# First norm of a decoder step: k-tiles 0 and 1 as two stages of their own with half granules, and the other k-tiles scaled on GpSimd

## The chip, the core and the metric

The kernel runs on one core of a Trainium2 chip. The metric is device microseconds of one execution, the median of several runs. TensorE (PE) does the matmuls, VectorE (DVE), ScalarE (ACT) and GpSimd (POOL) the elementwise work, and SyncE (SP) issues most of the DMA transfers.

## What is computed

One step of a recurrent decoder layer for 256 prompt tokens and 32 sample tokens (8 sequences of 4), 288 columns in all, in fp32. The part that the change touches is the beginning:

```python
mod = jax.nn.silu(c) @ P['w_ada'] + P['b_ada']
sh1, sc1, gt1, sh2, sc2, gt2 = [m[:, None, :] for m in jnp.split(mod, 6, axis=-1)]
xn = rmsnorm(x, P['g_norm1']) * (1.0 + sc1) + sh1
mix, st = mixer(xn, states[l], P)      # begins with proj = xn @ P['w_in']
```

`x` has 2048 features, 16 k-tiles of 128. `c` has nine rows (one for the prompt, eight for the samples), and `w_ada` is 2048 x 12288; of it the first norm needs the columns of `sc1` and `sh1`, 32 MB. The three mixer branches, the output projection, a second norm, a feed-forward part of width 8192 and a last norm follow.

## The kernel before

Features lie on partitions and tokens along the free axis. Every large product is a `stream` (L160): four PSUM tiles of 128 output features x 288 columns, fed by granules of the weight. A granule is two k-tiles by 512 output features, 512 KB. `fetch` (L151) issues its DMA on SyncE and then splits it: ScalarE writes the rounded `hi` (L156), VectorE the rest `lo = raw - hi` (L157). For each k-tile and each of the four output tiles there are three matmuls: hi by xh (L171), hi by xl (L172), lo by xh (L173); xh and xl are the same split of the input. raw, hi and lo have three buffers each. SyncE issues in program order; the order on the other engines is made by a scheduler from priorities, `issue_after` and a simulated time line.

The first norm is not finished before the streams begin. The weights of `sc1` and `sh1` come in 32 units of 1 MB (`first`, L317), ordered by stages: `STAGES` (L26) gives for each stage the k-tiles whose modulation it needs. Stage 0 is k-tiles 0 and 1 (4 units), then 2 and 3 (4 units), 4 to 7, 8 to 11, 12 to 15 (8 units each). A unit's product (L275) is many small matmuls into one PSUM tile; the last unit of a stage is followed by `by_feature` (a transpose, L237) and `ada_finish` (L297, L300), which write `mod`. `modulate` (L404) then scales and shifts the stage's k-tiles in place, prompt columns by L409, sample columns by L412, and splits them into xh (L420) and xl (L421).

Per stage, six streams run (`early`: the projections for q, k, v and the first branch), each over the k-tiles of this stage alone. In stage 0 the PSUM tile is copied to its slot by VectorE and ScalarE in turn (`first_part`, L467), and in all later stages VectorE adds it (`plus_slot`, L472). Between two granules a pattern of letters (L477) says what is put in: L loads the next unit, V multiplies (visits) all units that are loaded, a point does nothing. A stage asserts that its units were visited.

Ahead of all this, squares of x are summed (L430, L432, L434), `rs` is the reciprocal root (L391 to L395), and VectorE multiplies x by `rs` in five instructions (L442), k-tiles 0-1, 2-3, 4-7, 8-11 and 12-15. Four units are loaded with the first granule behind the third, and visited one by one (L455 to L461). The tile `par` of small parameters comes in one transfer on GpSimd's queue (L95), of `con` only `eye` at first; the rest of `con` is loaded by GpSimd after a copy that waits for `mod` (L488 to L490).

Of the kernel before, what the change touches and what calls it, by code (L numbers as in the profile page):

```python
# [8 lines left out]
F32 = mybir.dt.float32  # L9
F32R = mybir.dt.float32r  # L10
AF = mybir.ActivationFunctionType
ALU = mybir.AluOpType
# [12 lines left out]
SH1, SC1, GT1, SH2, SC2, GT2 = range(6)  # L25
STAGES = [(0, 2, 0), (2, 4, 4), (4, 8, 8), (8, 12, 16), (12, 16, 24)]  # L26
NPRE = 6
# [3 lines left out]
          ("glo", 128), ("causal", 128), ("bdm", 128), ("hsel", 4), ("head", 4), ("half", 2)]  # L31
PARAMS = [("lcw", 32), ("lcb", 8), ("mcw", 32), ("mcb", 8), ("ba", 8), ("bx", 8), ("lam", 8),
# [21 lines left out]
def trunk(ctx, tc, io):  # L54
# [39 lines left out]
    par = cp.tile([P, PW], F32, tag="par", name="par")  # L94
    G.dma_start(par, io["par"])  # L95

# [48 lines left out]
    def weight_tiles():  # L145
        at["n"] += 1
        return [weight_tile(n) for n in ("raw", "hi", "lo")]
# [3 lines left out]
    def fetch(w, blk, g, kg=2, ahead=True):  # L151

        with tc.high_priority() if ahead else nullcontext():
            raw, hi, lo = (t.rearrange("p (k m) -> p k m", k=kg) for t in weight_tiles())
            Q.dma_start(raw, w[blk, g].rearrange("p (k m) -> p k m", k=kg))
            pace["hi"] = S.activation(hi, raw, AF.Copy)  # L156
            pace["lo"] = V.tensor_tensor(out=lo, in0=raw, in1=hi.bitcast(F32), op=ALU.subtract)  # L157
        return hi, lo

    def stream(w, blk, act, kt, evac, g0=0, width=512, ahead=True, k0=0, kg=2):  # L160
# [3 lines left out]
        for g in range(k0 // kg, kt // kg):  # L164
            hi, lo = fetched.pop(0) if fetched else fetch(w, blk, g0 + g, kg, ahead)
            for m in range(nm_t):
# [237 lines left out]
    def modulate(k0, k1, step):  # L404

        for k in range(k0, k1, step):
            x, r = (xa, xb)[k // 8][:, k % 8:k % 8 + step], slice(k, k + step)
# [31 lines left out]
    rs = inv_sqrt(row("lf"), ps[:, :N], bias=eps, scale=1.0 / (32 * D))  # L439
    for k, n in ((0, 2), (2, 2), (4, 4), (8, 4), (12, 4)):  # L440
        t = (xa, xb)[k // 8][:, k % 8:k % 8 + n, :]
        V.tensor_tensor(out=t, in0=t, in1=rs.unsqueeze(1).to_broadcast([P, n, N]), op=ALU.mult)  # L442

# [10 lines left out]

    slots.update(ids=(8, 9, 2, 3), n=0)  # L455
    for i in range(4):
        if i == 3:
            fetched.append(fetch(win, B_Q, 0))
        load_one()
    for i in range(4):  # L460
        visit(1)  # L461
# [8 lines left out]
    def plus_slot(dst, base):  # L470
        def f(m, p):
            V.tensor_tensor(out=dst[:, base + m, :], in0=dst[:, base + m, :], in1=p, op=ALU.add)  # L472
        return f


    slots.update(ids=(4, 5, 6, 7, 3, None, "st"), n=0)
    for i, p in enumerate((". L L L LV .", "L LL LL LV LLV .", "L L . L LV . L L . LLV . .", "L L . L LV . L L . LLV . .", "L L L L . V . L L . V .")):  # L477
        k0, k1, _ = STAGES[i]
        assert i < 4 or not held
        if i == 4:  # L480
            slots.update(ids=(3, 4, None, 5, 6, 7), n=0)
        every(p)
        assert f"first{i}" in done
        with tc.high_priority():
            modulate(k0, k1, 2 if i else 1)
        if i == 0:
            a, w = COFF["eye"]
            for r in (slice(0, a), slice(a + w, CW)):  # L488
                G.tensor_copy(con[:, r.start:r.start + 1], mod[:, SC1, 0, 0:1])
                G.dma_start(con[:, r], io["con"][:, r])  # L490
# [1108 lines left out]
```

## Time and profile before

| | us |
|---|---|
| median of 3 runs | 1980.41 |
| lowest and highest | 1979.29, 1980.63 |
| profiled execution, its own time | 1981.87 |
| its span | 1980.1 |
| TensorE busy in the span | 1942.9 |

A row of the timeline gives the start, the duration, the engine, the line of the kernel, the operation with out<-in and shape, a count where like instructions follow each other, and in brackets the idle time of the engine ahead of it with what ended it. Durations overlap where an engine is pipelined; the distance of two starts is then the price of one. PEclk is the granted TensorE clock as a share of 2.4 GHz.

### The profile page before, as it was taken

The page shows a single profiled execution, that of the slowest core. Times are in us where ns is not written, and L with a number is a line of the kernel's source. Part 1 is how long each engine was busy: PE and PEld are TensorE (multiplying, and loading weights), DVE is VectorE, ACT ScalarE, POOL GpSimd, SP SyncE. Part 2 cuts the span into 40 slices and gives each one's busy share as a digit, 9 for nine tenths or more (in the row PEclk, how much of TensorE's full clock was granted, in tenths as well). Part 3 has the DMA queues.
Part 4 walks back from the last instruction along what each step waited for, and adds up shares of the span by engine and source line. Part 5 has one row for each costly group of instructions (what it writes and reads, how often), then busy time and mean ns, then how long its engine had stood idle before and what let it go on. Part 6 is the DMA issues. An engine that isn't in the chain of part 4 may idle for free.

```text
span 1980.1 us, 35638 instructions
## 1 busy us (share of the span) xinstructions
PE 1942.9 (98%) x14944; PEld 1839.8 (93%) x14944; DVE 1048.5 (53%) x1582; ACT 810.8 (41%) x1128; POOL 233.7 (12%) x319
## 2 busy tenths in 40 slices
PE   6999999999999999999999999999999999999997
PEld 5899989998999998799999999999999999999997
DVE  5665747545673456554444564444444445454565
ACT  4232464535454344243333454443333334343433
POOL 0000200000133021101013331000000001010101
PEclk8999999999999999999999999999999999999999
DMA  9887757537543358957778645444444444444443
GB/s 381 331 306 287 293 196 271 205 140 263 186 152 134 122 180 274 313 202 276 276 280 348 245 146 191 160 166 163 173 170 160 160 164 172 168 162 166 160 162 120
DMA packets 109569, 416.99 MB, mean 211 GB/s; under 512 B 11569, under 2 KB 11745, under 8 KB 105697
## 3 DMA queue, kind: packets, MB, share of 16 engines
q1 hardware_dynamic: 100368, 382.34, 52.5%
q0 software_dynamic: 8032, 28.99, 4.4%
q10 hardware_dynamic: 1008, 3.39, 0.5%
q8 instruction: 117, 1.92, 0.4%
q14 instruction: 44, 0.35, 0.1%
HBM read 397.86 MB, written 16.81 MB: 209 GB/s over the span
## 4 chain that ended last, share of the span: by engine, by line
PE 95%; DMA 3%; DVE 1%; issue 1%; ACT 0%; SPq 0%; DVEq 0%; POOL 0%; ACTq 0%; POOLq 0%
PE mm L171 28%; PE mm L173 28%; PE mm L172 28%; PE pa L275 4%; DMA raw<-win 2%; PE px L1256 0%; PE pi L1248 0%; DMA st<-gla 0%; DVE lo L157 0%; PE px L573 0%; DMA s<-mC 0%; PE px L804 0%; PE px L1183 0%; PE px L128 0%; PE px L652 0%
## 5 line engine op out<-in xcount | busy, mean ns | idle before, releaser
L157 DVE TENSOR_TENSOR lo<-raw,hi 128x1024 fp32r<-128x1024 f32 x450 | 555.8, 1237 | 545.6 <-ACT hi L156 528.1
L156 ACT ACTIVATE hi<-raw 128x1024 fp32r<-128x1024 f32 x450 | 476.9, 1061 | 826.4 <-PE mm L172 621.7
L171 PE MATMUL mm<-xh,hi 128*128 128x288 f32 x2576 | 763.2, 300 | 6.4 <-ACT xh L420 6.2
L172 PE MATMUL mm<-xl,hi 128*128 128x288 f32 x2576 | 760.2, 297 | 0.1
L173 PE MATMUL mm<-xh,lo 128*128 128x288 f32 x2576 | 744.7, 296 | 0.7 <-DVE lo L157 0.6
L171 PEld LDWEIGHTS mm<-xh,hi 128*128 128x128 f32 x2576 | 483.6, 189 | 26.1 <-issue 9.9
L171 PE MATMUL mm<-s,hi 128*128 128x288 f32 x1664 | 490.7, 297 | 0.3 <-ACT s L936 0.3
L172 PEld LDWEIGHTS mm<-xl,hi 128*128 128x128 f32 x2576 | 486.3, 189 | 2.7 <-issue 0.9
L172 PE MATMUL mm<-s,hi 128*128 128x288 f32 x1664 | 488.6, 295 | 0.0
L173 PEld LDWEIGHTS mm<-xh,lo 128*128 128x128 f32 x2576 | 481.5, 189 | 3.3 <-DVE lo L157 1.4
L173 PE MATMUL mm<-s,lo 128*128 128x288 f32 x1664 | 476.4, 295 | 0.4 <-DVE lo L157 0.4
L171 PEld LDWEIGHTS mm<-s,hi 128*128 128x128 f32 x1664 | 311.8, 188 | 5.7 <-issue 4.6
L172 PEld LDWEIGHTS mm<-s,hi 128*128 128x128 f32 x1664 | 312.5, 188 | 0.8 <-issue 0.5
L173 PEld LDWEIGHTS mm<-s,lo 128*128 128x128 f32 x1664 | 308.3, 188 | 1.3 <-DVE lo L157 0.7
L157 DVE TENSOR_TENSOR lo<-s,hi 128x1024 fp32r<-128x1024 f32 x80 | 98.0, 1225 | 113.8 <-ACT hi L156 113.8
L156 ACT ACTIVATE hi<-s 128x1024 fp32r<-128x1024 f32 x80 | 85.0, 1062 | 140.7 <-PE mm L172 140.0
L1432 POOL TENSOR_TENSOR t<-t 128x288 f32<-128x288 f32 x64 | 60.2, 951 | 639.2 <-ACT t L1431 639.2
L472 DVE TENSOR_TENSOR s<-s,mm 128x288 f32<-128x288 f32 x96 | 41.8, 451 | 41.3 <-PE mm L173 40.4
L275 PE MATMUL pa<-s,silc 128*32 128x128 f32 (+2 forms) x720 | 53.3, 411 | 5.9 <-DMA s<-wad 5.9
L1448 DVE TENSOR_TENSOR s<-s,mm 128x288 f32<-128x288 f32 x96 | 40.3, 451 | 33.8 <-PE mm L173 32.6
L955 POOL TENSOR_TENSOR s<-s,t 128x288 f32<-128x288 f32 x32 | 30.8, 989 | 190.3 <-DVE t L954 190.2
L275 PEld LDWEIGHTS pa<-s,silc 128*32 128x32 f32 x720 | 21.8, 112 | 23.6 <-issue 10.3
(379 smaller groups left out, 1123.4 us busy)
## 6 DMA issues: line engine op xcount, KB each, us to landing
raw<-win SPq DMA_DIRECT2D x192, 512.0 KB, 4.7
raw<-wf SPq DMA_DIRECT2D x176, 512.0 KB, 4.1
s<-wf SPq DMA_DIRECT2D x80, 512.0 KB, 3.3
s<-wada SPq DMA_DIRECT2D x26, 1024.0 KB, 8.8
s<-wad SPq DMA_DIRECT2D x24, 1024.0 KB, 8.5
ag<-wada SPq DMA_DIRECT2D x22, 1024.0 KB, 5.5
raw<-wout SPq DMA_DIRECT2D x32, 512.0 KB, 5.7
st<-wada SPq DMA_DIRECT2D x20, 512.0 KB, 7.6
```

What stands on the lines that cost most here:

```text
L156: pace["hi"] = S.activation(hi, raw, AF.Copy)
L157: pace["lo"] = V.tensor_tensor(out=lo, in0=raw, in1=hi.bitcast(F32), op=ALU.subtract)
L171: T.matmul(pss[m][:, :N], hi[:, kk, ms], xh, start=k == k0, stop=False)
L172: T.matmul(pss[m][:, :N], hi[:, kk, ms], xl, start=False, stop=False)
L173: pace["last"] = T.matmul(pss[m][:, :N], lo[:, kk, ms], xh, start=False, stop=k == kt - 1)
L275: pace["prod"] = T.matmul(ps[32 * j:32 * j + 32, h * w // 4:(h + 1) * w // 4], silu_c(k), v[:, j], start=k == 0 and h == 0, stop=k == KT - ...
L472: V.tensor_tensor(out=dst[:, base + m, :], in0=dst[:, base + m, :], in1=p, op=ALU.add)
L955: G.tensor_tensor(out=a, in0=a, in1=t, op=ALU.add)
L1432: G.tensor_tensor(out=r, in0=r, in1=r, op=ALU.mult)
L1448: V.tensor_tensor(out=a, in0=a, in1=p, op=ALU.add)
```

## The change

Stage 0 becomes two stages, k-tile 0 and k-tile 1, of 2 units each (a unit holds eight of the reduction tiles for 256 columns instead of four for 512). In these two stages a granule is one k-tile, half as large, in the first half of the raw, hi and lo buffers. `fetch` now only issues the DMA; the split is a function `halve`, called where the granule is used. Two units instead of four are visited ahead of the first stream, and the first two half granules are fetched behind them; the second is split after the modulation of k-tile 0.

For k-tile 0 `modulate` has a path of its own: sample columns on VectorE, xh of the prompt columns on ScalarE directly from `mod`, and then the in-place scaling and xl on VectorE. The scaling by `rs` is one VectorE instruction for k-tile 0 and 15 GpSimd instructions for the others. The second stage evacuates odd output tiles by a ScalarE copy and a GpSimd addition (`plus_half`). The patterns are new; in the third stage (k-tiles 2 and 3) the last visit stands after the last of the six streams. `par` is reordered, 112 of its columns are loaded first and the rest with the rest of `con`.

```diff
-STAGES = [(0, 2, 0), (2, 4, 4), (4, 8, 8), (8, 12, 16), (12, 16, 24)]
+STAGES = [(0, 1, 0), (1, 2, 2), (2, 4, 4), (4, 8, 8), (8, 12, 16), (12, 16, 24)]
...
-    G.dma_start(par, io["par"])
+    G.dma_start(par[:, 0:112], io["par"][:, 0:112])
...
-            raw, hi, lo = (t.rearrange("p (k m) -> p k m", k=kg) for t in weight_tiles())
-            Q.dma_start(raw, w[blk, g].rearrange("p (k m) -> p k m", k=kg))
+            if kg == 1:
+                raw, hi, lo = (t[:, 0:512].unsqueeze(1) for t in weight_tiles())
+                src = w[blk, g // 2][:, 512 * (g % 2):512 * (g % 2) + 512].unsqueeze(1)
+            else:
+                raw, hi, lo = (t.rearrange("p (k m) -> p k m", k=kg) for t in weight_tiles())
+                src = w[blk, g].rearrange("p (k m) -> p k m", k=kg)
+            Q.dma_start(raw, src)
+        return raw, hi, lo, ahead
+
+    def halve(raw, hi, lo, ahead):
+
+        with tc.high_priority() if ahead else nullcontext():
             pace["hi"] = S.activation(hi, raw, AF.Copy)
             pace["lo"] = V.tensor_tensor(out=lo, in0=raw, in1=hi.bitcast(F32), op=ALU.subtract)
         return hi, lo
...
+        if k0 == 0:
+            x, xs = xa[:, 0], xa[:, 0, NP:N].rearrange("p (b t) -> p b t", b=NB)
+            for kind, op in ((SC1, ALU.mult), (SH1, ALU.add)):
+                V.tensor_tensor(out=xs, in0=xs, in1=mod[:, kind, 0, 1:9].unsqueeze(2).to_broadcast([P, NB, TS]), op=op)
+            S.activation(xh[:, 0, 0:NP], x[:, 0:NP], AF.Identity, bias=mod[:, SH1, 0, 0:1], scale=mod[:, SC1, 0, 0:1])
+            S.activation(xh[:, 0, NP:N], x[:, NP:N], AF.Copy)
+            V.tensor_scalar(x[:, 0:NP], x[:, 0:NP], mod[:, SC1, 0, 0:1], mod[:, SH1, 0, 0:1], ALU.mult, ALU.add)
+            pace["mod"] = V.tensor_tensor(out=xl[:, 0], in0=x, in1=xh[:, 0].bitcast(F32), op=ALU.subtract)
+            return
...
-    for k, n in ((0, 2), (2, 2), (4, 4), (8, 4), (12, 4)):
+    def normalize(e, k, n):
         t = (xa, xb)[k // 8][:, k % 8:k % 8 + n, :]
-        V.tensor_tensor(out=t, in0=t, in1=rs.unsqueeze(1).to_broadcast([P, n, N]), op=ALU.mult)
+        e.tensor_tensor(out=t, in0=t, in1=rs.unsqueeze(1).to_broadcast([P, n, N]), op=ALU.mult)
+
+    with tc.high_priority():
+        normalize(V, 0, 1)
+    for k in range(1, KT):
+        normalize(G, k, 1)
...
-    slots.update(ids=(8, 9, 2, 3), n=0)
-    for i in range(4):
-        if i == 3:
-            fetched.append(fetch(win, B_Q, 0))
+    slots.update(ids=(8, 9), n=0)
+    for i in range(2):
         load_one()
-    for i in range(4):
+    fetched.append(halve(*fetch(win, B_Q, 0, 1)))
+    fetched.append(fetch(win, B_Q + 1, 0, 1))
+    for i in range(2):
         visit(1)
...
+    def plus_half(dst, base):
+        def f(m, p):
+            if m % 2:
+                t = t288()
+                S.copy(t, p)
+                G.tensor_tensor(out=dst[:, base + m, :], in0=dst[:, base + m, :], in1=t, op=ALU.add)
+            else:
+                V.tensor_tensor(out=dst[:, base + m, :], in0=dst[:, base + m, :], in1=p, op=ALU.add)
+        return f
...
-    for i, p in enumerate((". L L L LV .", "L LL LL LV LLV .", "L L . L LV . L L . LLV . .", "L L . L LV . L L . LLV . .", "L L L L . V . L L . V .")):
+    load_one()
+    for i, p in enumerate((". . L V L .", "L . LV L V .", "L L LLV LL LV LV", "L L . L LV . L L . LLV . .", "L L . L LV . L L . LLV . .", "L L L L . V . L L . V .")):
...
-            run(stream(win, b, act1, k1, (plus_slot if i else first_part)(dst, base), k0=k0))
+            run(stream(win, b, act1, k1, (first_part, plus_half, plus_slot)[min(i, 2)](dst, base), k0=k0, kg=min(2, k1 - k0)))
```

## Rows read from the trace of the kernel before

**Rows 1.** The page: its first line, and TensorE's busy tenths in 40 slices.

```profile
span 1980.1 us, 35638 instructions
...
PE   6999999999999999999999999999999999999997
```

**Rows 2.** Windows of 10 us: busy time by engine, clock, DMA share, GB/s.

```profile
20.00:30.00 10.00, 3.37 (x38) 2.82 (x39) 6.09 (x16) 2.89 (x5) 1.50 (x4) 0.50 1.02 415
30.00:40.00 10.00, 10.00 (x66) 10.00 (x66) 5.89 (x9) 3.90 (x7) 0.00 (x0) 0.84 1.02 397
80.00:90.00 10.00, 7.11 (x33) 6.20 (x32) 8.14 (x21) 3.38 (x4) 0.00 (x0) 0.72 1.00 393
90.00:100.00 10.00, 10.00 (x73) 10.00 (x72) 4.73 (x8) 3.08 (x3) 0.00 (x0) 0.94 0.78 306
```

**Rows 3.** TensorE's waits from 0 to 300 us: total, times, longest.

```profile
PE mm L171 <- ACT xh L420: 6.2, 2, 3.5
```

**Rows 4.** Timeline of TensorE from 0 to 32 us.

```profile
15.29 1.08 PE L275 MATMUL pa<-s,silc 128*32 128x128 f32 x32 [0.23 <-DMA s<-wad]
...
23.10 1.93 PE L275 MATMUL pa<-s,silc 128*32 128x128 f32 x32 [4.22 <-DMA s<-wad]
28.56 1.33 PE L171 MATMUL mm<-xh,hi 128*128 128x288 f32 x4 [3.53 <-ACT xh L420]
...
30.17 0.44 PE L171 MATMUL mm<-xh,hi 128*128 128x288 f32 x1
30.41 0.44 PE L172 MATMUL mm<-xl,hi 128*128 128x288 f32 x1
```

**Rows 5.** DMA issues around 1.7 us: KB each, us to landing.

```profile
par<-par POOLq DMA_DIRECT2D x1, 277.0 KB, 6.0
```

**Rows 6.** Timeline of VectorE from 14 to 30 us.

```profile
15.71 5.23 DVE L442 TENSOR_TENSOR s<-s,row 128x576 f32<-128x576 f32 x5
...
25.10 0.32 DVE L237 STREAM_TRANSPOSE t<-pa 128x128 f32<-128x128 f32 x1 [3.01 <-PE pa L275]
25.43 1.23 DVE L157 TENSOR_TENSOR lo<-raw,hi 128x1024 fp32r<-128x1024 f32 x1
26.57 0.26 DVE L297 TENSOR_TENSOR mod<-t,par 128x18 f32<-128x18 f32 x2
```

**Rows 7.** Timeline of TensorE from 62 to 92 us.

```profile
81.32 0.29 PE L172 MATMUL mm<-xl,hi 128*128 128x288 f32 x1
81.45 0.29 PE L173 MATMUL mm<-xh,lo 128*128 128x288 f32 x1
84.38 1.09 PE L171 MATMUL mm<-xh,hi 128*128 128x288 f32 x3 [2.64 <-ACT xh L420]
...
86.33 0.61 PE L172 MATMUL mm<-xl,hi 128*128 128x288 f32 x1
```

**Rows 8.** Timeline of VectorE from 48 to 110 us.

```profile
50.57 0.32 DVE L237 STREAM_TRANSPOSE t<-pa 128x128 f32<-128x128 f32 x1 [1.05 <-PE pa L275]
...
53.78 0.76 DVE L421 TENSOR_TENSOR xl<-s,xh 128x576 fp32r<-128x576 f32 x1 [0.20 <-ACT xh L420]
...
80.28 0.45 DVE L237 STREAM_TRANSPOSE t<-pa 128x256 f32<-128x256 f32 x1
```

**Rows 9.** VectorE's instructions from 28 to 110 us, by line and shape.

```profile
L157 DVE TENSOR_TENSOR lo<-raw,hi 128x1024 fp32r<-128x1024 f32 x18 | 22.0, 1222 | 10.8 <-ACT hi L156 10.6
L472 DVE TENSOR_TENSOR s<-s,mm 128x288 f32<-128x288 f32 x34 | 14.9, 452 | 15.2 <-PE mm L173 14.9
```

**Rows 10.** Timeline of VectorE from 227 to 236 us.

```profile
227.17 4.72 DVE L524 SCALAR_TENSOR_TENSOR s<-s,par,s 128x255 f32<-128x255 f32 x6
```

**Rows 11.** Timeline of GpSimd from 227 to 236 us.

```profile
228.14 0.84 POOL L515 TENSOR_TENSOR s<-s,par 128x256 f32<-128x256 f32 x1
```

**Rows 12.** Line 524, all its instructions: duration in ns, least, median, most.

```profile
L524 DVE SCALAR_TENSOR_TENSOR s<-s,par,s x48: 469/481/1424, 218.7 to 586.7; 128x255 f32<-128x255 f32 x16, 128x254 f32<-128x254 f32 x16, 128x253 f32<-128x253 f32 x16
```

**Rows 13.** Line 955, all its instructions on GpSimd, likewise.

```profile
L955 POOL TENSOR_TENSOR s<-s,t x32: 791/810/1868, 612.4 to 1028.0; 128x288 f32<-128x288 f32 x32
```

More of the change, by code (lines that the diff above doesn't have):

```diff
@@ L31 @@
           ("glo", 128), ("causal", 128), ("bdm", 128), ("hsel", 4), ("head", 4), ("half", 2)]
-PARAMS = [("lcw", 32), ("lcb", 8), ("mcw", 32), ("mcb", 8), ("ba", 8), ("bx", 8), ("lam", 8),
[1 row of a table removed]
+PARAMS = [("bada", 96), ("g1", 16), ("lcw", 32), ("lcb", 8), ("mcw", 32), ("mcb", 8), ("ba", 8), ("bx", 8), ("lam", 8),
[1 row of a table added]
           ("h0", 64), ("bi", 1), ("bf", 1), ("m0", 8),
@@ L164, in stream @@
         for g in range(k0 // kg, kt // kg):
-            hi, lo = fetched.pop(0) if fetched else fetch(w, blk, g0 + g, kg, ahead)
+            got = fetched.pop(0) if fetched else fetch(w, blk, g0 + g, kg, ahead)
+            hi, lo = got if len(got) == 2 else halve(*got)
             for m in range(nm_t):
@@ L473, in plus_slot @@
         return f
+    def plus_half(dst, base):
[7 more added lines that the diff above has]
+        return f
     slots.update(ids=(4, 5, 6, 7, 3, None, "st"), n=0)
-    for i, p in enumerate((". L L L LV .", "L LL LL LV LLV .", "L L . L LV . L L . LLV . .", "L L . L LV . L L . LLV . .", "L L L L . V . L L . V .")):
+    load_one()
+    for i, p in enumerate((". . L V L .", "L . LV L V .", "L L LLV LL LV LV", "L L . L LV . L L . LLV . .", "L L . L LV . L L . LLV . .", "L L L L . V . L L . V .")):
         k0, k1, _ = STAGES[i]
-        assert i < 4 or not held
-        if i == 4:
+        assert i < 5 or not held
+        if i == 5:
             slots.update(ids=(3, 4, None, 5, 6, 7), n=0)
@@ L484, in trunk @@
         with tc.high_priority():
-            modulate(k0, k1, 2 if i else 1)
+            modulate(k0, k1, 2 if i > 1 else 1)
         if i == 0:
             a, w = COFF["eye"]
-            for r in (slice(0, a), slice(a + w, CW)):
-                G.tensor_copy(con[:, r.start:r.start + 1], mod[:, SC1, 0, 0:1])
-                G.dma_start(con[:, r], io["con"][:, r])
+            for t, n, r in ((con, "con", slice(0, a)), (con, "con", slice(a + w, CW)), (par, "par", slice(112, PW))):
+                G.tensor_copy(t[:, r.start:r.start + 1], mod[:, SC1, 0, 0:1])
+                G.dma_start(t[:, r], io[n][:, r])
+        if i == 0:
+            with tc.issue_after(pace["mod"].ins):
+                fetched[-1] = halve(*fetched[-1])
         for b, dst, base in early:
-            run(stream(win, b, act1, k1, (plus_slot if i else first_part)(dst, base), k0=k0))
+            run(stream(win, b, act1, k1, (first_part, plus_half, plus_slot)[min(i, 2)](dst, base), k0=k0, kg=min(2, k1 - k0)))
     visit()
```

2 rows, old and new, of the table PARAMS are left out of this document.

## The prediction

> **What bounds the kernel now.** I read four views, from coarse to fine. The page first: the span is 1980.1 us and TensorE is busy in nine tenths or more of nearly every slice; only the first slice (49.5 us) and the last show less [rows 1]. So a change to the first norm can only pay in the first 90 us or so, and whatever it saves there is kept, because what follows is TensorE in a row. The 10 us windows show where: in 20 to 30 us TensorE has 3.37 us of work and the granted clock is at its lower level (0.50), while the DMA engines are full (share 1.02, 415 GB/s); the other hole is 80 to 90 us [rows 2]. The list of waits names both holes: TensorE waits 6.2 us, in two pieces, for xh, the modulated input of a stage [rows 3].
>
> The timeline shows what xh waits for. Unit 1 of the conditioning weights was multiplied at 15.29; the fourth, on which stage 0 depends, at 23.10, after 4.22 us of waiting for its DMA; the first matmul of the stream stands at 28.56 [rows 4]. Between the two lies a chain on VectorE: transpose at 25.10, then the split of a weight granule that got in between (25.43 to 26.57), then mod, the scaling, xh [rows 6]. So the start is bound by four megabytes of weights coming in behind the input at the DMA's full rate, plus 3.46 us of chain. At 415 GB/s a unit of 1.05 MB is 2.5 us.
>
> The second hole: TensorE's last matmul of the stage for k-tiles 2 and 3 starts at 81.45, three isolated ones follow at 84.38, and it runs on only from 86.33 [rows 7]. The chain there starts with the transpose at 80.28 [rows 8].
>
> **The sum** is made on the profiled execution, 1981.87 us (span 1980.1 and 1.8 around it); the median of the runs is 1980.41, so a saving worked out in the one is taken off the other. I compare the time from 0 to the point where the stage for k-tiles 4 to 7 runs, 86.33; behind it the instructions are the same.
>
> **Part 1, the start: two units instead of four, half a granule, a shorter chain.** Stage 0 now needs k-tile 0 alone: 2 units. The second lies in place at about 15.2 (its product at 15.29 had waited for it [rows 4]). The first par transfer shrinks from 277 KB [rows 5] to 57 KB, at most 0.5 us earlier. The product is 1.08 us [rows 4]; it has twice the matmuls at half the columns, so half to twice that; I take the same, and the end at 16.1. The granule of 256 KB lands behind it and is split before the chain needs it. The chain was 25.10 to 28.56, 3.46 us; without the granule's split in its middle (1.14) it is 2.3 [rows 4, 6]; one k-tile instead of two, and ScalarE making xh straight from mod, I put at 0.4 less: 1.9, first matmul at 18.0. That is the lower end.
>
> It has a price: the other scalings, 5.23 us on VectorE in five instructions [rows 6], become 15 on GpSimd from 15.7 on. One such instruction is 0.81 us (median of 32 of the same form) [rows 13], so they run to 27.9 at least, beside this chain. How the two engines go together is seen at 227 us: six VectorE instructions with two inputs in SBUF take 4.72 us, 0.79 each, beside a GpSimd that runs one elementwise instruction after the other [rows 10, 11]; alone the median is 0.48 [rows 12]. Every one is held up by 0.31. Short ones could wait for a whole GpSimd instruction, some 0.6 more. On the chain are five of that kind (two for mod, one for its gain, two for the sample columns): 1.6 to 3.0 us; the split of the half granule can add up to 1.4. So the first matmul comes between 18.0 and 22.4. I take 20.6, near the end that the 227 us rows give. Saved: 28.56 less 20.6 is **8.0** (6.2 to 10.6).
>
> The Trainium skill says this more harshly (SBUF — State Buffer, Who interferes with whom): a VectorE instruction with two SBUF inputs and a GpSimd instruction that reads SBUF fully block each other, the second to issue waiting for the first. The rows at 227 us agree that they collide, but show 0.31 us and not a whole GpSimd instruction as the price of one; by the rule in full the start would be at the 22.4 end.
>
> **Part 2, what moves behind the first matmul.** The products of units 2 and 3 stood before it and now stand among the streams: 2 x 1.0, **+2.0** (1 to 4.3). Stage 0's twelve half granules (two stages of six) do the work of the six whole ones before; matmuls are equal in number, 0.13 us apart at the full clock [rows 7].
>
> The waits between stages: from transpose to the end of xl it took 50.57 to 54.54, 4.0 us [rows 8]. In the kernel before, a full stream of 24 matmuls, 3.2 us, lay over it: 0.8 uncovered. In the new second stage the last product comes one half stream (1.6 us) ahead of the next stage: 2.4 uncovered, **+1.6**, with GpSimd's additions beside it up to 4.0 (+3.2); at least 1.8 (+1.0). From the first to the second stage two half streams (3.2) cover a chain for one k-tile, while GpSimd ends its scalings: **+0.5** (0 to 2.0).
>
> Into the stage for k-tiles 4 to 7 the last visit now follows the last stream, with nothing over it. Before, in spite of a stream over it, TensorE lost 81.58 to 86.33, 4.7 us, since two splits and several sums stood on VectorE among the chain [rows 7, 8, 9]. Now SyncE has the granules there long before, and VectorE has only the chain: 3.2 (the 4.0 with no 0.45 sums in it); **-1.5** (-1.7 to +1.3).
>
> The clock: stage 0 ran at the lower level, 0.24 us a matmul [rows 4], until the 30 to 40 window (0.84), and once more after 86.33 (0.94 in 90 to 100) [rows 2]. What is lost is the time by the missing share of the clock: 1.44 x 0.5 and 10 x 0.16 the first time, 3.67 x 0.5 and 10 x 0.06 the second, 2.3 to 2.4 each. TensorE still idles some 4 us ahead of stage 0 and 3 us ahead of k-tile 4: both falls stay, no term.
>
> **VectorE in the half streams.** Per half stream it has two sums of 0.45 and half a split, 0.6 of 1.22 [rows 9]: 1.5 against 12 x 0.13, 1.6, of TensorE. That fits only without the collisions; the products of units 2 to 7 give it air. In the second stage every other sum goes over ScalarE and GpSimd, two additions of 0.81 per half stream: 1.6, just as tight. **+0.6** (0 to 4).
>
> **DMA.** Up to the last unit of k-tiles 4 to 7 the bytes are those of before, less what is late in par and con; the input's 2.4 MB, 16 units of 1.05 and 6.3 MB of granules, 25.5 MB, are 61.5 us at 415 GB/s, and with the slower start they land by 66 to 68 us; TensorE asks for that unit at some 77, in case (a) below after 70. SyncE issues in program order and stays at most three granules ahead of the splits; of half granules that is fewer bytes, but 1 MB units stand between them in its queue. Half granules of 2 KB rows are shown nowhere; if each took as long as a whole one, 12 x 0.6 = 7 us, it would still be in time. On GpSimd the copies and transfers for the rest of con and par now queue behind the scalings, some 3 us later than before; they serve work beside much later streams. No term.
>
> Sum: -8.0 + 2.0 + 1.6 + 0.5 - 1.5 + 0.6 = **-4.8 us**, 1980.4 less 4.8: **1975.6 us**.
>
> **Rivals.** (a) The collisions cost nothing on the chain: GpSimd gives way, the start is at 18.0 and TensorE idles so little that the clock stays up for stage 0. Saved 10.6 and 2.3; added 2.0 + 1.0 - 1.5: 11.4 less, 1969.0. For it: the chain's instructions are short. Against: rows 10. (b) Given back: start at 22.4 (6.2 saved), added 2.0 + 3.2 + 1.0 + 0.5, and nothing won before k-tile 4: 1980.9, no difference. This is also what the skill's rule in full would make of it. (c) **Slower**: VectorE becomes the bound of the half stages. With 0.31 a split it needs 1.84 per half stream, over TensorE's 1.6, and from there on every half stream is late; 12 of them cost 3 to 6, I take 4. Then 0 to 1 costs 2.0, 1 to 2 costs 3.2 and lets the clock fall once more (2.3), 2.0 for the products: 13.5 added, 6.2 saved, 1987.7. It decides if GpSimd is busy through the whole second stage. Against: the products leave gaps. (d) The change doesn't bring the start forward: the units' products are ordered behind other work, or the split of the granule stands before mod as it did; first matmul at 24.5, saved 4.1 against 3.2: 1979.5.
>
> **How the numbers follow.** Forecast 0.42 (1971.5 to 1979.5 by its own bounds), (a) 0.27, (b) 0.13, (c) 0.13, (d) 0.05. About 0.2%, 4 us, is what a measurement of this kernel can tell from no change, so faster means under 1976.4: (a) and six tenths of the forecast, 0.53; slower (c), 0.13; the rest 0.34. The range reaches halfway into (a) and (c): 1968 to 1985.
>
> **What would show it.** Right: first stream matmul between 18 and 22.4; VectorE's chain instructions near 0.8 us beside GpSimd; a wait for xh or xl of 2 to 3 us into k-tiles 2 and 4; the stage for k-tile 4 at 80 to 83. Wrong: a start after 23, a wait over 1 us inside a half stage for a sum or a split, a clock under 0.9 between 35 and 70 us, or a difference behind 100 us, which would mean that the order of later work changed.

## The result, and the profile after

The changed kernel takes 1987.8 us (median of 8 runs) against 1980.5 for the kernel before in the same session: a ratio of 1.0032, interval 1.0023 to 1.0041, so 0.32% slower: 7.3 us between the medians, 6.3 by the ratio, which I use from here on. The profiled execution took 1985.0 us, its span 1983.2.

On the page of the changed kernel TensorE's busy tenths answer to [rows 1]: the first slice rises from 6 to 7 tenths, the second falls from 9 to 8.

```profile
PE   7899999999999999999999999999999999999997
```

The windows [rows 2], here TensorE's busy time, clock, DMA share and GB/s alone, and TensorE's waits from 0 to 300 us [rows 3]:

```profile
20.00:30.00 10.00, 9.15 (x41) 0.60 0.78 288
...
50.00:60.00 10.00, 5.89 (x40) 0.77 1.01 418
60.00:70.00 10.00, 10.00 (x86) 0.89 1.02 417
...
90.00:100.00 10.00, 9.34 (x51) 0.68 0.58 211
```

```profile
PE mm L182 <- ACT xh L440: 8.8, 2, 4.7
...
PE mm L182 <- ACT xh L422: 4.5, 1, 4.5
```

Where there were two waits of 6.2 us for xh, there are now 8.8 us into later stages (L440) besides 4.5 for the first one (L422), and the clock is down in three places instead of two: 0.60 in 20 to 30 us, 0.77 in 50 to 60, 0.68 in 90 to 100 (mixtures of its two levels, 1.2 and 2.4 GHz; a matmul of the stream is 0.24 us from the next at the lower, 0.13 at the upper). TensorE's timeline, to be laid beside [rows 4] and [rows 7]:

```profile
20.12 1.33 PE L182 MATMUL mm<-xh,hi 128*128 128x288 f32 x4 [4.46 <-ACT xh L422]
...
34.50 0.29 PE L184 MATMUL mm<-xh,lo 128*128 128x288 f32 x1
35.88 0.29 PE L182 MATMUL mm<-xh,hi 128*128 128x288 f32 x1 [1.09 <-DVE s L432]
...
51.75 0.29 PE L184 MATMUL mm<-xh,lo 128*128 128x288 f32 x1
56.15 1.33 PE L182 MATMUL mm<-xh,hi 128*128 128x288 f32 x4 [4.11 <-ACT xh L440]
57.27 0.44 PE L183 MATMUL mm<-xl,hi 128*128 128x288 f32 x1
```

```profile
84.89 1.07 PE L286 MATMUL pa<-st,silc 128*32 128x256 f32 x16
90.66 1.33 PE L182 MATMUL mm<-xh,hi 128*128 128x288 f32 x4 [4.70 <-ACT xh L440]
91.79 0.44 PE L183 MATMUL mm<-xl,hi 128*128 128x288 f32 x1
```

Two groups of VectorE's chain at the start, the gain of mod and the sample columns, with GpSimd busy beside them; first the like of them in the kernel before, behind the last row of [rows 6], then after:

```profile
26.78 0.18 DVE L300 SCALAR_TENSOR_TENSOR mod<-mod,par 128x18 f32<-128x18 f32 x1
...
27.32 0.18 DVE L412 TENSOR_TENSOR s<-s,mod 128x32 f32<-128x32 f32 x1
```

```profile
17.56 0.72 DVE L311 SCALAR_TENSOR_TENSOR mod<-mod,par 128x9 f32<-128x9 f32 x1
18.32 1.48 DVE L420 TENSOR_TENSOR s<-s,mod 128x32 f32<-128x32 f32 x2
```

The start came where it was forecast: 20.12 instead of 28.56. But TensorE then stands still between 34.50 and 35.88, 51.75 and 56.15, and from the product at 84.89 to 90.66, and runs on only at 91.79, where the kernel before did at 86.33: 5.5 us behind, after having been 8.4 ahead. Both waits into later stages have the same picture on VectorE; [rows 8] is what they were costed from:

```profile
50.39 0.32 DVE L248 STREAM_TRANSPOSE t<-pa 128x128 f32<-128x128 f32 x1 [0.17 <-PE pa L286]
50.74 1.35 DVE L308 TENSOR_TENSOR mod<-t,par 128x18 f32<-128x18 f32 x2
52.01 0.44 DVE L507 TENSOR_TENSOR s<-s,mm 128x288 f32<-128x288 f32 x1
52.38 0.46 DVE L311 SCALAR_TENSOR_TENSOR mod<-mod,par 128x18 f32<-128x18 f32 x1
...
53.20 0.45 DVE L507 TENSOR_TENSOR s<-s,mm 128x288 f32<-128x288 f32 x1
...
54.02 1.22 DVE L167 TENSOR_TENSOR lo<-raw,hi 128x1024 fp32r<-128x1024 f32 x1
55.16 0.22 DVE L432 TENSOR_TENSOR s<-s,mod 128x64 f32<-128x64 f32 x1
56.13 0.76 DVE L441 TENSOR_TENSOR xl<-s,xh 128x576 fp32r<-128x576 f32 x1 [0.75 <-ACT xh L440]
```

```profile
86.03 0.45 DVE L248 STREAM_TRANSPOSE t<-pa 128x256 f32<-128x256 f32 x1 [0.34 <-PE pa L286]
...
88.54 1.22 DVE L167 TENSOR_TENSOR lo<-raw,hi 128x1024 fp32r<-128x1024 f32 x1
89.68 0.35 DVE L432 TENSOR_TENSOR s<-s,mod 128x64 f32<-128x64 f32 x2
```

Times are counted below from the start of the last matmul ahead of a gap to the next one's: 4.40 us at 51.75, 5.08 from the last of the product's sixteen. At 54.02 and at 88.54 the split of a granule (L167, 1.22 us) stands between the last scalings and the one shift that xh still waits for. This granule is the second of the stage; nobody needs it yet. In front of 54.02 two sums (0.44 and 0.45) are in the chain too, and two of its instructions for mod take 1.35 us.

### The profile page after: what moved, and what is told of

The parts are those of the page before. It is cut to its first block, busy times and chain, and to the rows that moved or that the text cites. A ratio compares the mean times of both kernels' runs of the same rounds, so it can differ in the third digit from the quotient of the medians.

```text
span 1983.2 us, 36011 instructions
## 1 busy us (share of the span) xinstructions
PE 1944.3 (98%) x15072; PEld 1841.9 (93%) x15072; DVE 1056.4 (53%) x1600; ACT 814.8 (41%) x1147; POOL 256.8 (13%) x348
## 4 chain that ended last, share of the span: by engine, by line
PE 92%; DMA 4%; DVE 2%; issue 1%; ACT 0%; POOL 0%; SPq 0%; DVEq 0%; POOLq 0%; ACTq 0%
PE mm L182 28%; PE mm L184 27%; PE mm L183 27%; PE pa L286 4%; DMA raw<-win 2%; DMA o_C_s<-s 1%; DMA o_C_s<-st 1%; DVE lo L167 1%; PE px L612 0%; PE px L843 0%; PE px L1222 0%; PE px L128 0%; PE px L691 0%; DMA s<-mC 0%; PE pi L1287 0%
## 5 line engine op out<-in xcount | busy, mean ns | idle before, releaser
L167 DVE TENSOR_TENSOR lo<-raw,hi 128x1024 fp32r<-128x1024 f32 (+1 forms) x456 | 558.5, 1226 | 533.4 <-ACT hi L166 509.0
L166 ACT ACTIVATE hi<-raw 128x1024 fp32r<-128x1024 f32 (+1 forms) x456 | 477.7, 1048 | 820.2 <-PE mm L183 623.6
L167 DVE TENSOR_TENSOR lo<-s,hi 128x1024 fp32r<-128x1024 f32 x80 | 98.0, 1225 | 113.8 <-ACT hi L166 113.8
L286 PE MATMUL pa<-s,silc 128*32 128x64 f32 (+3 forms) x832 | 52.3, 372 | 0.8 <-DMA s<-wad 0.8
L441 DVE TENSOR_TENSOR s<-t,s 128x288 fp32r<-128x288 f32 x64 | 33.8, 567 | 15.5 <-ACT s L440 15.5
```

Source lines behind the costliest of these rows:

```text
L286: pace["prod"] = T.matmul(ps[32 * j:32 * j + 32, h * w // 4:(h + 1) * w // 4], silu_c(k), v[:, j], start=k == 0 and h == 0, stop=k == KT - ...
L441: V.tensor_tensor(out=dst_l[:, r], in0=src[:, r], in1=dst_h[:, r].bitcast(F32), op=ALU.subtract)
```

## The experiments

I had three theories. **A:** the chains into k-tiles 2 and 4 lie bare and are longer than forecast, since other VectorE work is ordered into them, and each long idle stretch makes the clock fall. **B:** VectorE and GpSimd hold each other up, in the scalings and in the second stage's sums. **C:** half granules fill whole buffers, SyncE runs out of them, and bytes are missing later. All ratios are to the kernel before, run in turn on the same chip; 0.001 is 2.0 us. Each ratio is known to 0.0009 or little more to either side, so the times alone tell two runs apart from a difference of some 0.0013 on, 2.5 us; a smaller one has to be read from the traces, and each trace is of one execution.

**The changed kernel again**, to know what a repetition is worth.

> The changed kernel once more, for a second trace and the scatter of its time. Both theories: median 1986 to 1989 us. If the scatter of 6 us among its eight runs comes from TensorE's clock, runs that are 3 us slower must show a mean granted clock about 0.0015 lower; if it comes from waits, the clock is the same and the waits into k-tiles 2 and 4 (4.3 and 4.7 us in the first trace) differ.

1.0028 (1.0019 to 1.0038). The loss stands; from here I take 1.0030, 5.9 us, for the changed kernel. As to the scatter, in both sets of eight runs the mean granted clock is some 0.0008 to 0.0009 lower where a run is 3 us slower (0.992 at 1985.0, 0.989 and 0.990 at 1990.9 and 1991.2): the clock explains more than half of it. The second trace has the same two gaps, of 5.02 us at 53.13 and of 5.1 ahead of 91.40, but the lower clock lasts 10.3 us behind the start, 3.3 behind the first gap and 4.2 behind the second, where the first trace has 8.0, 6.1 and 5.7. Its windows behind the first gap:

```profile
50.00:60.00 10.00, 5.27 (x57) 4.68 (x56) 8.50 (x15) 4.38 (x8) 5.40 (x5) 0.90 1.01 408
60.00:70.00 10.00, 10.00 (x78) 9.61 (x81) 6.76 (x14) 1.06 (x1) 0.00 (x0) 0.93 1.02 418
```

**Theory B at the start:** the other scalings back on VectorE.

```diff
-    for k in range(1, KT):
-        normalize(G, k, 1)
+    for k, n in ((1, 1), (2, 2), (4, 4), (8, 4), (12, 4)):
+        normalize(V, k, n)
```

> The scaling of k-tiles 1 to 15 goes back to VectorE, in five instructions; all else as changed. Theory A (thin cover: the loss is the uncovered chains into k-tiles 2 and 4 and the clock that falls there): these two waits stay, the 5.2 us of scaling only move, 1985 to 1990 us. Theory B (collision: GpSimd beside VectorE makes the chains and the splits late): first stream matmul at 18 instead of 20.1 us, no split of a half granule over 0.7 us, 3 to 5 us less than the changed kernel, 1983 us.

1.0037 (1.0025 to 1.0049). TensorE's timeline: the first matmul comes later, not sooner.

```profile
21.92 1.33 PE L182 MATMUL mm<-xh,hi 128*128 128x288 f32 x4 [5.94 <-ACT xh L422]
```

Without GpSimd beside it the chain itself, from the transpose at 20.47 to the first matmul, takes 1.45 us instead of 3.34 (16.78 to 20.12), so its company costs this chain 1.9 us. But the scalings, 5.30 us from 14.64 on, now stand ahead of the chain on VectorE, and cost more. The other way round, **the kernel before with GpSimd's scalings** (all but k-tiles 0 and 1):

```diff
-        V.tensor_tensor(
+        (G if k else V).tensor_tensor(
```

> The kernel before with k-tiles 2 to 15 scaled by 14 GpSimd instructions and nothing else changed. Theory B: the chain from the last product (25.1 us) to the first matmul (28.6) runs beside GpSimd until some 28 and grows by 1 to 2 us: 1982 to 1983.5 us. Theory A: VectorE is rid of 4.5 us of scaling and the first split no longer stands behind it, but the fourth unit's DMA still sets the start: within 1 us of before.

1.0010 (1.0001 to 1.0019): 2.0 us lost. TensorE's first matmul and VectorE's chain, to be laid beside [rows 4] and [rows 6]:

```profile
29.86 1.33 PE L171 MATMUL mm<-xh,hi 128*128 128x288 f32 x4 [5.32 <-ACT xh L420]
```

```profile
24.61 0.32 DVE L237 STREAM_TRANSPOSE t<-pa 128x128 f32<-128x128 f32 x1 [2.97 <-PE pa L275]
...
26.31 0.85 DVE L297 TENSOR_TENSOR mod<-t,par 128x18 f32<-128x18 f32 x2
27.10 0.74 DVE L300 SCALAR_TENSOR_TENSOR mod<-mod,par 128x18 f32<-128x18 f32 x1
```

The two instructions for mod took 0.26 us together and take 0.85, the gain 0.74. The chain from the transpose to the first matmul takes 5.25 us (24.61 to 29.86) instead of 3.46. So B is real, with a price of 1.8 us on a chain of this kind, and the forecast's start had it in.

**Theory B in the second stage:** all its sums on VectorE.

```diff
-(first_part, plus_half, plus_slot)[min(i, 2)](dst, base)
+(plus_slot if i else first_part)(dst, base)
```

> The second stage's sums all on VectorE; ScalarE's copies and GpSimd's additions of that stage go. Theory B (collision): mod's instructions ahead of k-tile 2 (0.58, 0.85 and 0.46 us beside GpSimd) return to 0.16 to 0.2, the wait of 4.4 falls to some 3, 1 to 3 us less. Theory A: VectorE gets 12 more sums of 0.37, the chain waits for these instead; within 1 us of the changed kernel, or 1 to 2 us more.

1.0032 (1.0020 to 1.0045), no better, and TensorE's wait into k-tiles 2 grows to 5.37 us (ahead of 58.86). The split of the second granule stands in its chain again:

```profile
55.77 1.23 DVE L167 TENSOR_TENSOR lo<-raw,hi 128x1024 fp32r<-128x1024 f32 x1 [1.59 <-ACT hi L166]
```

The three instructions for mod do return to 0.16, 0.17 and 0.18 us, as B says. But four sums now stand among them instead of two, and behind the sums this split comes ahead of the scalings: VectorE idles 1.59 us for ScalarE's hi and then splits for 1.23. So this run shows the collision, and does not show what it would be worth without the sums and the split.

**Theory A, the covers:** a stream laid over the chain into k-tiles 2 and 3, over that into k-tiles 4 to 7, and over both.

```diff
-"L . LV L V .", "L L LLV LL LV LV"
+"L . LLV . . .", "L L LLV LL LV LV"
...
+"L . LV L V .", "L L LLV LL LLV ."
...
+"L . LLV . . .", "L L LLV LL LLV ."
```

> In the second stage the last unit is loaded and multiplied with the three before it, after the third half stream, so that three half streams (4.8 us) instead of one lie over the chain to k-tiles 2 and 3. Theory A: the wait of 4.3 us ahead of stage k-tile 2 falls to 0 to 1.5 and the clock doesn't fall there, 4 to 6 us less, 1982 to 1984 us. Theory B: the chain stays beside GpSimd's additions, the wait stays above 3 us, at most 1 us less.

> In the third stage the last two units are multiplied ahead of the last stream, which then lies over the chain to k-tiles 4 to 7, as in the kernel before. Theory A: the wait of 4.7 us there (5.8 to the steady matmuls) falls to some 2.5, and the clock falls less long: 3 to 5 us less, 1983 to 1985 us. Theory B: GpSimd has nothing to do in this stage and the wait is VectorE's own work, which stays: at most 1 us less.

> The two earlier visits together (second and third stage). If the covers add up: 0.9 and 2.1 us, 1983.5 us. Theory C (SyncE's queue): with the wait ahead of k-tile 2 gone, the third stage starts 3 us earlier and waits for a granule instead (2.1 us at 72 us in the run with the second stage alone), so the gain is that of the third stage alone or less, 1984 to 1986 us.

1.0024 (1.0015 to 1.0033), 1.0018 (1.0010 to 1.0027), and 1.0007 (0.9998 to 1.0016) with both. The waits behave as A says: with the first pattern only 1.0 us is left of the wait into k-tiles 2 and 3, with the second 3.0 instead of 5.1 us of the last gap. The time does not follow: 1.2 and 2.4 us are won, neither clear of the noise, where A expected 4 to 6 and 3 to 5. With the first pattern TensorE waits for a granule at 73.73 instead, and its last gap grows to 5.8 us (84.1 to 89.90). And with both TensorE has a new wait, for a granule that came late, after a window from 40 to 50 us in which the DMA engines were half idle (columns of the windows: PE, PEld, DVE, ACT and POOL busy, clock, DMA share, GB/s):

```profile
75.43 0.40 PE L182 MATMUL mm<-xh,hi 128*128 128x288 f32 x1 [2.61 <-ACT hi L166]
```

```profile
40.00:50.00 10.00, 10.00 (x172) 9.33 (x172) 6.53 (x17) 4.83 (x12) 4.76 (x6) 1.00 0.55 197
70.00:80.00 10.00, 7.39 (x64) 6.31 (x67) 5.24 (x10) 1.06 (x1) 0.00 (x0) 1.00 1.03 416
```

**Theory C:** the same, with two half granules sharing a set of buffers, so that six may be under way.

```diff
+                if spare:
+                    raw, hi, lo = (t[:, 512:1024].unsqueeze(1) for t in spare.pop())
+                else:
+                    spare.append(weight_tiles())
+                    raw, hi, lo = (t[:, 0:512].unsqueeze(1) for t in spare[0])
```

> The changed kernel with a stream laid over the chains into k-tiles 2 and into k-tiles 4 (the two patterns of the earlier run that had both), and with two half granules sharing one set of raw, hi and lo buffers, so that six half granules instead of three may be fetched ahead. Theory C (with half granules in whole buffers SyncE runs dry of buffers and the DMA engines idle between 40 and 50 us, share 0.55, and the bytes are missing later): share in 40 to 50 us at 0.9 or more, the 2.90 us wait for hi at 72.53 gone, 2 to 3 us less than the run with both patterns: 1979 to 1981. If the DMA engines idle for another reason (the order of SyncE's queue itself): share below 0.7, the wait at 72 us stays above 2 us, 1982 to 1984.

1.0010 (1.0000 to 1.0019): no gain over the run before. C's mechanism is there, its price is not:

```profile
40.00:50.00 10.00, 9.86 (x172) 9.23 (x172) 8.10 (x17) 5.23 (x11) 6.26 (x9) 1.00 0.81 312
50.00:60.00 10.00, 7.20 (x35) 6.51 (x35) 6.85 (x13) 3.57 (x6) 3.39 (x4) 0.73 1.01 421
```

The share from 40 to 50 us rose from 0.55 to 0.81 and the wait of 2.90 us shrank to 0.90. In their place three waits of 1.0 to 1.6 us came between 50.9 and 55.5, and the clock fell (0.73). The late granule was not the last thing that was late.

**The clock:** idle matmuls, whose result nobody reads, in the two long gaps of the changed kernel.

```diff
+        if i in (2, 3):
+            wps = misc()
+            with tc.high_priority(), tc.issue_after(pace["last"].ins), tc.issue_after(pace["prod"].ins):
+                for _ in range(WARM[i]):
+                    T.matmul(wps[:, :N], xh[:, 0, 0:P], xh[:, 0, :], start=True, stop=True)
```

> The changed kernel with 30 and 32 extra matmuls (xh of k-tile 0 by itself, into a PSUM tile that nobody reads) behind the last work ahead of k-tiles 2 and 4: some 4 us of TensorE work in gaps of 4.4 and 5.1 us. Nothing of the chains on VectorE changes. If the fall of the clock is a good part of the loss (theory A, second half): the granted clock stays at 1.0 behind both gaps, 2.3 us less at each, 4 to 5 us less in all, 1982 us. If the clock falls anyway or falls where the loss isn't: within 1 us of the changed kernel, 1986 to 1988.

1.0015 (1.0006 to 1.0024): 3.0 us won on the changed kernel, less than expected. One reason is in the trace: the 32 idle matmuls of the last gap hold TensorE until 89.72, when the first xh had been there since 88.99. The clock is whole wherever it had fallen behind the start:

```profile
50.00:60.00 10.00, 8.78 (x86) 8.12 (x78) 7.31 (x16) 3.67 (x6) 4.91 (x5) 1.00 1.02 421
...
90.00:100.00 10.00, 10.00 (x77) 9.91 (x76) 6.47 (x10) 3.33 (x4) 0.00 (x0) 1.00 0.86 297
```

**The clock at the start** stayed low for 8 us in the changed kernel (20.12 to 28.1), 4.7 before. Here idle matmuls run ahead of the first stream and in the last gap, on the kernel with both covers and shared buffers; in the trace of that kernel without them it stayed low for 4.6 us (20.23 to 24.81).

```diff
+WARM = {0: 16, 3: 14}
...
+                    else:
+                        wh = fetched[0][0]
+                        T.matmul(wps[:, :N], wh[:, 0, 0:P], wh[:, 0, 0:N], start=True, stop=True)
```

> The kernel with shared half buffers and both patterns, and with idle matmuls whose result nobody reads: 16 while TensorE waits for the modulation of k-tile 0, 14 while it waits for k-tiles 4 to 7. Theory A (each idle stretch of 3 us or more costs the lower clock afterwards; the low clock after the start lasted 8 us in the changed kernel, which is 4 us lost): granted clock above 0.9 in 20 to 30 us instead of 0.6, 2 to 4 us less than without the idle matmuls, 1976 to 1979, which is faster than the kernel before. Rival: the stretch after the start is paced by VectorE and ScalarE (evacuations, splits beside GpSimd) and not by the clock: clock above 0.9, TensorE's waits grow by as much, less than 1 us gained.

1.0011 (1.0002 to 1.0020), the same as without them (1.0010). The window and the timeline, first without the idle matmuls, then with them:

```profile
20.00:30.00 10.00, 8.72 (x47) 7.63 (x48) 8.80 (x13) 4.63 (x12) 9.94 (x14) 0.81 1.03 407
```

```profile
24.57 0.40 PE L187 MATMUL mm<-xh,hi 128*128 128x288 f32 x1 [0.56 <-DVE s L497]
```

```profile
20.00:30.00 10.00, 7.46 (x58) 6.60 (x62) 9.09 (x14) 4.64 (x12) 9.94 (x14) 1.00 1.02 408
```

```profile
24.52 0.40 PE L188 MATMUL mm<-xh,hi 128*128 128x288 f32 x1 [1.46 <-DVE s L498]
...
33.65 0.31 PE L292 MATMUL pa<-s,silc 128*32 128x64 f32 x4 [1.82 <-issue]
```

The clock is 1.00 instead of 0.81 in 20 to 30 us, and TensorE waits longer for the same VectorE copy, 1.46 instead of 0.56 us: its next matmul starts at 24.52 instead of 24.57 (24.47 in the changed kernel). So up to there the rival holds: the first half streams are paced by their neighbours, and the low clock was free. What it costs the changed kernel between 24.5 and 28 us this run cannot show, since its base had the full clock back by then. The wait of 1.82 us in a product has no releaser in the profile and stays unexplained.

**The split in the chain**, the step that the trace of the changed kernel points to: the second granule's split is held until xl is written, in the third and fourth stage. Its transfer moves ahead of one unit each in SyncE's order; nothing else is changed.

```diff
+        if i in (2, 3):
+            held1 = halve(*fetch(win, B_Q, k0 // 2))
+            held2 = fetch(win, *((B_Q + 1, 1) if i == 2 else (B_Q, 3)))
         with tc.high_priority():
             modulate(k0, k1, 2 if i > 1 else 1)
+        if i in (2, 3):
+            fetched.append(held1)
+            with tc.issue_after(pace["mod"].ins):
+                fetched.append(halve(*held2))
```

> The changed kernel with one thing moved: the split of the second granule of the third and of the fourth stage is held until xl of the stage is written, so that it no longer stands in the middle of the chain. If the split in the chain is what made the waits longer than predicted (4.4 instead of 2.4 us and 5.85 instead of 3.2 us): gap 1 to 2 at 3.2 us, gap 2 to 3 at 3.9 us, 2 to 2.5 us less than the changed kernel, 1985.5 to 1986. If the split only changes places with work that is needed as early: gaps shorter, but a wait for lo of 1 us behind each, no difference, 1987.5 to 1988.5.

1.0012 (1.0003 to 1.0021): 3.6 us won. TensorE's timeline, the window after the first gap, and VectorE's timeline:

```profile
55.87 0.80 PE L182 MATMUL mm<-xh,hi 128*128 128x288 f32 x4 [2.89 <-ACT xh L440]
```

```profile
88.68 1.33 PE L182 MATMUL mm<-xh,hi 128*128 128x288 f32 x4 [3.56 <-ACT xh L440]
```

```profile
50.00:60.00 10.00, 7.11 (x66) 6.35 (x65) 8.71 (x17) 3.99 (x7) 4.55 (x5) 0.86 1.01 393
```

```profile
55.85 0.76 DVE L441 TENSOR_TENSOR xl<-s,xh 128x576 fp32r<-128x576 f32 x1 [0.75 <-ACT xh L440]
56.52 1.22 DVE L167 TENSOR_TENSOR lo<-raw,hi 128x1024 fp32r<-128x1024 f32 x1
```

The gaps, counted from the last matmul ahead of them (52.69 and 84.74), are 3.18 and 3.94 us instead of 4.40 and 5.08, as expected. They give 2.4 us. For the first gap this is more than the scatter of single executions: it is 3.2 to 3.8 us in the three traces that hold the split, and 4.4 to 5.5 in four that do not (the two of the changed kernel, those with idle matmuls alone and with the third stage's cover alone). The other 1.2 us of the 3.6 are within the noise. It is not shown that the shorter gap keeps the clock low for less long: the windows from 50 to 70 us lose 1.3 us to the lower clock here and 2.45 in the first trace of the changed kernel, but 1.2 in its second, whose gap is 5.02.

**Do the terms add?** The split held and idle matmuls together; then the same with a stream over the last chain.

```diff
+WARM = {2: 20, 3: 25}
...
+WARM = {2: 20, 3: 10}
-"L L LLV LL LV LV"
+"L L LLV LL LLV ."
```

> The changed kernel with the second granule's split held behind xl in the third and fourth stage, and idle matmuls (20 and 25) in the two gaps that remain. If the split in the chain (about 4 us) and the clock falls (about 2.7 us) are separate terms: 1980.5 to 1982, no difference from the kernel before. If both are one term (a gap short enough keeps the clock): 1984 to 1985, no better than the split alone.

> The same, with the last visit of the third stage one stream earlier, so that a stream lies over the chain into k-tiles 4 to 7, and 10 idle matmuls in what is left of that gap. If the uncovered chain is what the third stage's pattern costs: gap 2 to 3 of 1 to 1.5 us instead of 3.9, 2 us less than with the chain uncovered, 1978 to 1980. If the sums of the stream laid over it get into the chain as they did before the change: gap 2.5 to 3, 1980 to 1982.

1.0001 (0.9992 to 1.0009) and 0.9990 (0.9981 to 0.9999), both by their times as one of their two cases expected. In the second run the last gap, from the last matmul of the stream, is still 3.3 us (84.00 to 87.32), longer than either case: four sums of the covering stream are in the chain again, and a split with them (81.36, 1.18 us). The 2.2 us by the ratio are within the noise. Alone the split gave 3.6 and the clock 3.0, together 5.7 (1.0030 to 1.0001): with both mended the loss of the change is gone. The traces agree that these are two terms, at a point behind both gaps, the product of the next stage's four units: it begins at 110.94 in the changed kernel (110.98 in its second trace), at 109.17 with the split held, at 106.69 with idle matmuls and at 105.14 with both, so 1.8, 4.3 and 5.8 us earlier. With both the granted clock is 1.00 from 50 to 60 and from 90 to 100 us.

**The same in the kernel before**, whose chains hold a split at 25.43 and at 83.89: idle matmuls in its two gaps, the splits held, and both.

```diff
+WARM = {0: 14, 2: 18}
...
+        if i == 0:
+            rest = fetch(win, B_Q + 1, 0, now=False)
+        if i == 2:
+            fetched.append(fetch(win, B_Q, 2))
+            rest = fetch(win, B_Q, 3, now=False)
...
+        if i in (0, 2):
+            with tc.issue_after(pace["mod"].ins):
+                fetched.append(halve(*rest))
...
+WARM = {0: 12, 2: 14}
```

> The kernel before with idle matmuls alone: 14 while TensorE waits for the modulation of k-tiles 0 and 1, 18 while it waits for k-tiles 4 to 7. If the prediction's price of a clock fall (2.3 to 2.4 us each, time by the missing share of the clock) is right: the clock stays at 1.00 from 30 us on and 3.5 to 4.7 us are won, 1976 to 1978. If the lost clock lay beside other waits (the DMA of the later units): under 2 us won, 1979 to 1980.

> The kernel before, with the second granule's split held behind xl in the first stage and in the stage for k-tiles 4 to 7. If a split inside the chain costs the kernel before its length too: first matmul at 27.4 instead of 28.56, steady matmuls of k-tile 4 at 84 instead of 86.33 (less the 1.1 won at the start), 2 to 2.5 us less, 1979 to 1979.5. If the DMA's rate sets the pace behind the start anyway (the units of k-tiles 4 to 7 land no earlier): under 1 us.

> The kernel before with both: the splits held out of the chains and idle matmuls (12 and 14) in the two gaps. If the terms add: 2 us (the idle matmuls alone won that) and 2 us more, 1977 to 1978, faster than both kernels. If they are one term: 1979, as with the idle matmuls alone.

0.9990 (0.9981 to 0.9998), 0.9992 (0.9983 to 1.0000) and 0.9981 (0.9972 to 0.9990). Idle matmuls won 2.0 us, less than the price worked out for two falls; the held splits won 1.6; both 3.8. The 1.6 are hardly apart from nothing (the interval reaches 1.0000), and the three not clearly from one another; that the terms add fits these times, but is not shown by them. With the splits held the first matmul comes at 27.32 instead of 28.56, and that of k-tile 4 at 84.03:

```profile
27.32 1.33 PE L176 MATMUL mm<-xh,hi 128*128 128x288 f32 x4 [2.41 <-ACT xh L425]
...
84.03 0.79 PE L176 MATMUL mm<-xh,hi 128*128 128x288 f32 x4 [2.30 <-ACT xh L425]
```

Behind this gap of 2.30 us, without any idle matmul, the granted clock stays at 1.00 from 80 to 100 us (0.72 and 0.94 in [rows 2]). So in this kernel the held split takes the second fall of the clock away too, and what it wins there is not apart from the clock.

The kernel before with both, 1977.6 us, is the fastest of all: 3.8 us under the kernel before, 4.0 under the changed one with the same two mends (1.0001), and 1.8 under the best version of the changed one, which has a stream over its last chain besides; of these the 1.8 are not clear of the noise by the ratios. In both kernels the same two defects stood, and once they are mended the change wins nothing.

## Why the prediction was wrong, point by point

The ledger, from the two profiled executions, up to 86.33 before and 91.79 after (92.52 in the second trace of the changed kernel; its lower clock behind the first gap lasted half as long, so a single entry is good to some 1 us):

| term | forecast | measured |
|---|---|---|
| first matmul | -8.0 | -8.4 |
| products of units 2 and 3 | +2.0 | +1.9 (31.02 to 32.94) |
| VectorE in the half streams | +0.6 | +0.7 (waits of 0.24 and 0.49) |
| wait 0 to 1 | +0.5 | +1.25 (1.38 less 0.13) |
| wait 1 to 2 | +1.6 (2.4 less 0.8) | +4.3 (4.40 less 0.13; no wait there before [rows 3]) |
| third fall of the clock | 0 | +2.4 (57.27 to 62.08 at half) |
| low clock at the start | 0 | +1.4 (9.15 x 0.40 against 2.3) |
| wait into k-tile 4 | -1.5 | +1.2 |
| sum | -4.8 | +4.8 of 5.5 |

In the last wait 7.1 us pass from the matmul ahead of the product to 91.79, less 1.0 of product and five matmuls of 0.13: 5.5 lost, where before 4.9 less the same five, 4.2, were.

**Right:** the start, its chain and its price. I took 0.8 us for an instruction of the chain beside GpSimd; the gain and the two on the sample columns took 0.72 and 0.74, and the first matmul came within 0.5 of the forecast. Taking GpSimd's work to VectorE made it later, though the chain itself got shorter. The products and the half streams' tightness are right too.

**Wrong, first step: the wait 1 to 2, 2.4 us.** I took 4.0 us from transpose to the end of xl from one passage before [rows 8], and laid 1.6 over it; and I took 0.8 off for a wait in the kernel before that is not in its trace (its matmuls there start at 53.60 and 53.80). Measured are 6.5 (50.39 to 56.89) for the chain. Two sums were in the 4.0 already; new are the split, 1.1 net of overlap, and 1.4 for mod and its gain beside GpSimd's additions (1.35 and 0.46 instead of 0.27 and 0.18). In the second trace the chain is 7.1 (51.77 to 58.89), with 0.6 more at mod and its gain and 1.0 more at a scaling and a shift (0.83 and 0.81 instead of 0.41 and 0.22): where the collisions fall differs, their sum less so. The row at 25.43, a split inside the very chain I was reading [rows 6], was in front of me; I deducted it from the start and did not ask whether it would come back at the next stage.

**Wrong, second step: the wait into k-tile 4, 3.2 us,** with the reason that VectorE has only the chain there and SyncE the granules long before. The second half of the reason undid the first: because the granule was there early, its split was ready to be put into the chain, at 88.54. Holding it away gave 1.1 us of this wait (5.08 to 3.94) and 1.2 of the other; the remaining 0.7 over the forecast is the chain itself, which scales four k-tiles before the first xh where the one I had read scales two.

**Wrong, third step: the clock, "no term".** Only the two falls of before were counted, and the fall after 1 to 2 stood in rival (c) alone, where it went with a wait of 3.2. The wait was 4.1, and it fell. My way of pricing a fall, busy time by the missing share, is of the right size and rather an upper end: for the two falls behind the start the windows give 2.45 and 3.1 in the first trace, 1.2 and 2.9 in the second, and idle matmuls won 3.0 by the times, 4.3 by the traces; on the kernel before 2.0 and 2.4 of the 4.8 that I had worked out. The price itself differs from one execution to the next, which I had not allowed for. The low clock up to 24.5 us was free in the run that took it away; whether the +1.4 of the ledger was lost behind that or would else have been waited is open.

**The rival that came about** is (c) in its number, 1987.7, but not in its mechanism: the half streams were not late behind VectorE (0.7 us, not 4), and the start was not late. Its 1 to 2 and its fall of the clock were right in kind.

**DMA, "no term":** the DMA share fell to 0.78 and 0.76 (20 to 30 and 40 to 50 us) where the prediction expected the full rate. In the changed kernel TensorE waits for a DMA once, 0.8 us, ahead of the first stream; with the covers put back it waited for a late granule too, and bringing that earlier moved the wait elsewhere.

**What stays open.** Of the 5.5 us some 0.7 are in no term. How the gains of covers, buffers and clock would combine beyond the combinations shown was not tried. Behind 91.79 the profiled execution wins 2.3 back, but the medians lie 6.3 to 7.3 apart: single executions of one kernel differ by several microseconds (1985.0 to 1991.2 for the changed one). Part of this lies far behind the change: in 780 to 800 us the clock falls in the trace of the kernel before (0.94) and in the second of the changed one (0.91), and stays at 1.00 in the first. From the product of the next stage's four units to the end the changed kernel and its variants take 1870.9 to 1874.4 us. So the premise that whatever is saved ahead of 90 us is kept holds only to within some 4 us in a single execution: with the splits held the kernel before begins that product at 100.50 instead of 105.73, 5.2 us earlier, and ends only 1.3 earlier. Why is open.

## What to carry to other kernels

A chain of short instructions is as long as everything the scheduler may put into it: before costing an uncovered chain, list the work that is ready on its engine at that time (here the split of a weight that arrived early) and add it, or hold it back by an order of its own. A change that starts the work earlier but cuts it into more stages buys one gap and sells several; count for each new stage its chain, its cover, and the clock after it. And look first whether the defect that the new version exposes stands in the old one too: mending it there won 3.8 us, and the change none.

## What the runs showed of the hardware

VectorE beside GpSimd: I had costed 0.31 us an instruction. The timelines of the two engines in the changed kernel show something sharper:

```profile
18.98 0.79 POOL L462 TENSOR_TENSOR s<-s,row 128x288 f32<-128x288 f32 x1
```

```profile
19.10 0.71 DVE L420 TENSOR_TENSOR s<-s,mod 128x32 f32<-128x32 f32 x1
```

VectorE's instruction on 32 columns (0.18 us in the kernel without GpSimd's scalings) started 0.12 us after GpSimd's and ended at 19.81, 0.04 after its end at 19.77: it waited for nearly the whole rest. That is the rule of the Trainium skill (SBUF — State Buffer, Who interferes with whom), by which the second to issue waits for the first, and this trace agrees with it for the small instructions; the price is then the rest of GpSimd's instruction, so a chain of short ones goes at GpSimd's beat: the starts at 17.56, 18.32 and 19.10 are 0.76 and 0.78 apart, where GpSimd's instructions are 0.79 long. The 0.31 of [rows 10] came from instructions that take 0.48 alone [rows 12].

The granted clock: after 2.89 us of idle time (the run with the split held) it fell to the lower level (0.86 in 50 to 60 us); after 2.61 (both covers, 75.43) it stayed at 1.00 from 70 to 80. But the longest idle stretch does not decide alone: in the run with idle matmuls at the start it fell at 57.03, behind two waits of only 0.89 and 1.60 us (51.97 and 55.97), so a rule by its length alone, as in theory A of that run, is not what the rows show. And how long it stays low after the same kind of start differs: 8 us here (0.24 us a matmul from 20.12 until 28.0), 10.3 in the second execution of the same kernel, 4.7 in the kernel before.
